# Conformer convolution: first channel half moved between and beside the query/key projections of the second attention kind

## The chip, the cores and the metric

The kernel runs as one launch on one core of a Trainium2 chip. The time is device microseconds of one execution; a smaller one is better. The kernel before took 3023.3 us as the median of three runs (3010.88 to 3023.79).

## The reference, cut to what matters

Two transformer blocks are computed in float32, one after the other. The change lies in the first block, which has two layers (l = 0 and l = 1) over 512 main tokens and 256 context tokens of width 1024; layer 1 needs only the main tokens' result. One layer, cut:

```python
h = rms_norm(x, n1) * (1 + sc1) + sh1          # hc the same for the context
a_b, a_c, a_h, b_v, b_g, c_q, c_k, c_v, d_q, d_k, d_v = split_proj(h @ w_in)
ya = short_conv_mixer(a_b, a_c, a_h, conv_a)
yb = conformer_conv(b_v, b_g, conv_b, conv_b_bias, cln_g, cln_b)
yc = window_attention(apply_rope(q_heads(c_q), ...), ...)
yd = global_attention(apply_rope(rms_norm(q_heads(d_q), qn_g), ...), ...)
x_new = x + g1 * (concat([ya, yb, yc, yd]) @ w_out)
x_new = x_new + g2 * expert_choice_ffn(h2, ...)

def conformer_conv(a, g, w, bias, ln_g, ln_b):
    u = a * sigmoid(g)
    u = dwconv(u, w) + bias                    # depthwise, 31 taps, 256 channels
    return silu(layer_norm(u, ln_g, ln_b))
```

`c_q, c_k, c_v` are the queries, keys and values of the window attention (kind 0 in the kernel), `d_q, d_k, d_v` those of the global attention (kind 1). The 256 channels of the convolution are two halves of 128 (ch = 0 and 1), one partition a channel. The convolution needs nothing of the attention and the attention nothing of it; both end in `y`, which the output projection reads.

## The kernel before

The program is written with a tile framework: engines run their own queues in order, and the order of each queue is fixed when the kernel is built. A scheduler walks all instructions and gives an engine the ready one that stands first in program order, by its own model of durations; so an instruction that comes later in the program can run early, as filler, when all before it wait. Tiles come from pools: an instruction that needs a new tile waits until one of the pool's slots is free.

A matmul of float32 is made of three (`mm3`, L334 to L336): high part by high part, and the two mixed products, from operands split into a rounded high part and a rest. `take_hl` (L253 to L266) takes the next loaded weight tile and splits it: two casts on ACT (L263), two subtractions (L264) on DVE, or the second of them on POOL unless `dve` is set. The raw tile `w`, `wh` and `wl` are slots of one pool, `wp`, of six. Weights come through one list of entries in the order of use (`all_entries`) over SP's queue; `pump` keeps at most `cap` raw tiles issued and not released (2 in this stage).

A layer's first part runs so:

- `qkv_group` (L762): kind 0, then kind 1. Each kind has two weight tiles and six token tiles (four main, two context; I call such a step a position): 24 matmuls into a `pd` tile (a PSUM pool of two), which ACT copies out (L779, L783). For kind 1, DVE then works out the rms norm of the heads (a chain of small instructions, L788 to L793, with L278 to L280 in it) and the rotation (L808, L812), with POOL in between (L798, L816, L817); two positions later PE transposes the result (L826). Between the matmuls stand steps of the modulation vectors (`mods_steps`, L373), each on a 1 MB tile of `ada_w`: 24 in layer 0, 8 in layer 1.
- Attention: `attn_window`, `attn_global` and, in layer 0, `attn_ctx`, 8 units each (24 in layer 0, 16 in layer 1). A unit is scores (L935), maximum (L856), exponential (L862), sums and reciprocal (L866 to L870; L866 and L868 only where there is a sink), scaling of the probabilities (L881 on DVE for one head, L879 on ACT for the other), transposes (L907), copies out of PSUM (L330, L328), and the product with the values (L915).
- Beside it the conformer convolution, a Python generator: `long_conv` (L613). For ch = 0 and 1 and for each set of tokens (512 main, in layer 0 also 256 context): 48 matmuls (`two`, 24 for the values and 24 for the gate, two `pd` tiles), the gate (L625), the product `u` (L627), the middle tap (L630), and 30 further taps. Of those, 16 (14 for the context) are a product on ACT (L642) that POOL adds to `a2` (L644); the other 14 (16) are one instruction of DVE each (L648). POOL adds `a2` in the end (L650). `u`, `a2` and the taps' products share a pool `t2` of 6 slots in layer 0 and 8 in layer 1. From the seventh unit on three steps of the generator are emitted after each unit (START, RATE), and what is left after the last unit.
- `short_conv` (L679): three more weight tiles, each with the same 48 matmuls for each set, and the layer norm of the convolution's result. Then `out_proj`.

So in program order half 0 stands beside the units from the seventh on, and half 1, apart from its first instructions, behind all attention.

Of the kernel before, what the change touches and what calls it, by code (L numbers as in the profile page):

```python
# [1 line left out]

# [46 lines left out]
RATE = (3, 3)  # L49
BTA = 6  # L50
# [68 lines left out]
class Kern:  # L119
# [316 lines left out]
    def all_entries(self):  # L436
        for k in range(8):
            self.ada_entry(0, 0, k)
        for l in range(2):
# [5 lines left out]
            for x in ada[:cut]:  # L445
                self.ada_entry(*x)
            self.dense_entries("w_in", l, 7, 9, (4, 512))
            for x in ada[cut:]:
                self.ada_entry(*x)
            self.dense_entries("w_in", l, 0, 5, (8, 256))  # L450
# [67 lines left out]
    def layer(self, l):  # L518
# [42 lines left out]
        kq = self.qkv_group(l, hT, last, tiles, W)  # L561
        ep = self.phase(ptp=PT[l], p3p=P3[l], qsp=QS)
        sets = [(0, 512)] if last else [(0, 512), (1, 256)]
        conv = self.long_conv(l, hT, y, sets)
# [37 lines left out]
    def two(self, hT, w, m, n):  # L602

        out = []
        for q in range(2):
            pp = self.pd()
# [3 lines left out]
            out.append(pp)  # L610
        return out

    def long_conv(self, l, hT, y, sets):  # L613
# [3 lines left out]
        hb = self.sm(62, "hb", bufs=1)  # L617
        nc.vector.tensor_scalar(hb, self.pvv("cwb", l * 62, 62), 0.5, None, op0=ALU.mult)
        taps = lambda j, n: (slice(max(0, 15 - j), n - max(0, j - 15)), slice(max(0, j - 15), n - max(0, 15 - j)))
        for ch in range(2):  # L620
            w = self.take_hl(dve=WDVE)
            for m, n in sets:
                pv, pg = self.two(hT, w, m, n)
                th = self.t2((n,))
                nc.scalar.activation(out=th, in_=pg[:, :n], func=AF.Tanh, scale=0.5)  # L625
                u = self.t2((n,), s="u")
                nc.vector.scalar_tensor_tensor(u, th, 1.0, pv[:, :n], op0=ALU.add, op1=ALU.mult)  # L627
                ac = y[m](2 + ch)
                col = lambda j: hb[:, ch * 31 + j:ch * 31 + j + 1]
                nc.vector.tensor_scalar(ac, u, col(15), self.pvv("cbb", l * 2 + ch, 1), op0=ALU.mult, op1=ALU.add)  # L630
                yield

                side = SIDE if m == 0 else SIDEC
                for j in range(15 - side, 16 + side):
                    if j != 15:
                        to, fr = taps(j, n)
                        f = self.t2((n,), s="tap")[:, :to.stop - to.start]
                        if j == 15 - side:
                            a2 = self.t2((n,), s="a2")
                            nc.gpsimd.memset(a2[:, 0:16], 0.0)  # L640
                            f = a2[:, to]
                        nc.scalar.activation(out=f, in_=u[:, fr], func=AF.Copy, scale=col(j))  # L642
                        if j > 15 - side:
                            nc.gpsimd.tensor_tensor(a2[:, to], a2[:, to], f, op=ALU.add)  # L644
                            yield
                for j in list(range(15 - side)) + list(range(16 + side, 31)):
                    to, fr = taps(j, n)
                    nc.vector.scalar_tensor_tensor(ac[:, to], u[:, fr], col(j), ac[:, to], op0=ALU.mult, op1=ALU.add)  # L648
                    yield
                nc.gpsimd.tensor_tensor(ac, ac, a2, op=ALU.add)  # L650
# [102 lines left out]
    def qkv_group(self, l, hT, last, tiles, W):  # L753
# [14 lines left out]
        for kind in range(2):  # L768
            if kind == 1:
                W = [self.take_hl() for _ in range(2)]  # L770
            for it, (m, t) in enumerate(order):
# [67 lines left out]
                while done < goal:  # L839
                    next(steps)  # L840
                    done += 1
                MARK("qkv")
# [1278 lines left out]
```

## Time and profile before

| what | value |
|---|---|
| median of the runs | 3023.3 us (3010.88, 3023.3, 3023.79) |
| profiled execution, its own time | 3013.78 us |
| its span, first to last instruction | 3011.8 us |
| mean granted TensorE clock | 0.972 |
| busy share of the span | PE 94%, PEld 60%, DVE 42%, ACT 27%, POOL 15% |
| layer 0: kind 1 of the projections | about 98 to 157 us |
| layer 0: attention and convolution | about 157 to 332 us |
| layer 0: short convolution | about 332 to 385 us |
| layer 1: kind 1 | about 1113 to 1150 us |
| layer 1: attention and convolution | about 1150 to 1318 us |

The profiled execution's own time is 2 us over its span. PE is TensorE's matmuls, PEld its weight loads (which overlap the matmuls), DVE is VectorE, ACT ScalarE, POOL GpSimd, SP the queue of the weight transfers. Times in the rows below are us from the start of the span, durations us unless a row says ns. A clock of 1.00 is TensorE's full clock of 2.4 GHz, 0.50 is 1.2 GHz.

### The profile page before, as it was taken

The page shows a single profiled execution, that of the slowest core. Times are in us where ns is not written, and L with a number is a line of the kernel's source. Part 1 is how long each engine was busy: PE and PEld are TensorE (multiplying, and loading weights), DVE is VectorE, ACT ScalarE, POOL GpSimd, SP SyncE. Part 2 cuts the span into 40 slices and gives each one's busy share as a digit, 9 for nine tenths or more (in the row PEclk, how much of TensorE's full clock was granted, in tenths as well). Part 3 has the DMA queues.
Part 4 walks back from the last instruction along what each step waited for, and adds up shares of the span by engine and source line. Part 5 has one row for each costly group of instructions (what it writes and reads, how often), then busy time and mean ns, then how long its engine had stood idle before and what let it go on. Part 6 is the DMA issues. An engine that isn't in the chain of part 4 may idle for free.

```text
span 3011.8 us, 38597 instructions
## 1 busy us (share of the span) xinstructions
PE 2822.7 (94%) x15736; PEld 1802.0 (60%) x15736; DVE 1279.5 (42%) x2657; ACT 819.9 (27%) x1519; POOL 464.4 (15%) x378
## 2 busy tenths in 40 slices
PE   6989899999999879997999888999999999999998
PEld 3666675444444356674433224788886777888886
DVE  5387754111111157744222225532446483444344
ACT  3266432000000035631000003322236442322222
POOL 2233332111111024331000000222210001100000
PEclk9999899999999989998999999999999999999999
DMA  7710136999999942147999996232231122222222
GB/s 274 273 66 15 43 112 258 411 406 404 394 405 386 362 148 96 43 186 288 426 426 426 426 426 266 86 111 84 91 103 57 68 83 89 93 97 98 84 91 77
DMA packets 103841, 623.13 MB, mean 207 GB/s; under 512 B 11056, under 2 KB 13232, under 8 KB 36592
## 3 DMA queue, kind: packets, MB, share of 16 engines
q1 hardware_dynamic: 89120, 580.82, 48.7%
q0 software_dynamic: 8352, 18.10, 2.3%
q10 hardware_dynamic: 6192, 21.75, 1.9%
q8 instruction: 124, 2.03, 0.3%
q14 instruction: 53, 0.43, 0.0%
HBM read 601.74 MB, written 18.87 MB: 206 GB/s over the span
## 4 chain that ended last, share of the span: by engine, by line
PE 44%; DMA 7%; DVE 3%; ACT 1%; issue 0%; SPq 0%; DVEq 0%; ACTq 0%
PE pd L334 6%; PE pd L335 5%; PE pd L336 5%; PE pb L1242 4%; PE pb L334 3%; PE pa L334 3%; PE pb L335 3%; PE pb L336 3%; PE pa L335 3%; PE pa L336 3%; DMA w<-w_up 3%; PE pd L1279 2%; DMA w<-w_down 2%; DMA w<-w_gate 2%; PE pb L1337 1%; PE pb L1813 1%
## 5 line engine op out<-in xcount | busy, mean ns | idle before, releaser
L1242 PE MATMUL pb<-w,X 128*64 128x512 f32 x2048 | 464.3, 600 | 13.5 <-DMA w<-w_up 7.3
L1242 PEld LDWEIGHTS pb<-w,X 128*64 128x64 f32 x2048 | 150.9, 138 | 310.2 <-issue 268.5
L263 ACT CAST wh<-w 128x1024 fp32r<-128x1024 f32 (+3 forms) x239 | 235.9, 1029 | 360.2 <-issue 125.2
L1279 PE MATMUL pd<-w,hT 128*64 128x512 f32 (+1 forms) x2048 | 303.5, 493 | 6.0 <-DVE hT L330 2.6
L264 DVE TENSOR_TENSOR wl<-w,wh 128x1024 fp32r<-128x1024 f32 (+3 forms) x189 | 229.8, 1236 | 146.7 <-ACT wh L263 140.0
L334 PE MATMUL pd<-hh,wh 128*128 128x512 f32 (+1 forms) x720 | 284.6, 396 | 8.0 <-ACT wh L263 3.9
L336 PE MATMUL pd<-hh,wl 128*128 128x512 f32 (+1 forms) x720 | 283.0, 393 | 0.3 <-DVE wl L264 0.3
L335 PE MATMUL pd<-hl,wh 128*128 128x512 f32 (+1 forms) x720 | 282.9, 393 | 0.0
L1252 ACT ACTIVATE s<-pb 128x512 f32<-128x512 f32 x32 | 19.1, 598 | 694.4 <-PE pb L1242 694.4
L1279 PEld LDWEIGHTS pd<-w,hT 128*64 128x64 f32 (+1 forms) x2048 | 102.4, 123 | 165.7 <-issue 131.7
L264 POOL TENSOR_TENSOR wl<-w,wh 128x1024 fp32r<-128x1024 f32 (+1 forms) x50 | 132.0, 2639 | 412.4 <-ACT wh L263 390.1
L1253 DVE TENSOR_TENSOR s<-s,pb 128x512 f32<-128x512 f32 x32 | 22.0, 687 | 399.5 <-ACT s L1252 399.5
L334 PEld LDWEIGHTS pd<-hh,wh 128*128 128x128 f32 x720 | 138.4, 192 | 38.1 <-ACT wh L263 7.1
L336 PEld LDWEIGHTS pd<-hh,wl 128*128 128x128 f32 x720 | 138.1, 192 | 28.9 <-issue 0.8
L335 PEld LDWEIGHTS pd<-hl,wh 128*128 128x128 f32 x720 | 138.4, 192 | 28.0 <-issue 1.5
L334 PE MATMUL pb<-wh,fh 128*128 128x512 f32 x352 | 138.4, 397 | 0.8 <-DVE x L1674 0.8
L336 PE MATMUL pa<-hh,wl 128*128 128x512 f32 x352 | 139.1, 395 | 0.0
L334 PE MATMUL pa<-hh,wh 128*128 128x512 f32 x352 | 139.1, 395 | 0.0
L335 PE MATMUL pa<-hl,wh 128*128 128x512 f32 x352 | 139.1, 395 | 0.0
L335 PE MATMUL pb<-wl,fh 128*128 128x512 f32 x352 | 138.1, 392 | 0.0
L336 PE MATMUL pb<-wh,fl 128*128 128x512 f32 x352 | 138.1, 392 | 0.0
L1210 POOL DMA_INDIRECT gat<-xd,gi x48 | 47.0, 979 | 573.8 <-PE pa L1224 325.7
(464 smaller groups left out, 4698.1 us busy)
## 6 DMA issues: line engine op xcount, KB each, us to landing
w<-w_up SPq DMA_DIRECT2D x128, 1024.0 KB
w<-w_gate SPq DMA_DIRECT2D x128, 1024.0 KB
w<-w_down SPq DMA_DIRECT2D x128, 1024.0 KB
w<-ada_w SPq DMA_DIRECT2D x48, 1024.0 KB
w<-w_in SPq DMA_DIRECT2D x18, 1024.0 KB
w<-f1g SPq DMA_DIRECT2D x11, 1024.0 KB
w<-f1u SPq DMA_DIRECT2D x11, 1024.0 KB
w<-f2g SPq DMA_DIRECT2D x11, 1024.0 KB
```

What stands on the lines that cost most here:

```text
L263: nc.scalar.copy(hi[:, s], w[:, s])
L264: (nc.gpsimd if i and not (dve or self.dve) else nc.vector).tensor_tensor(lo[:, s], w[:, s], hi[:, s].bitcast(F32), op=ALU.subtract)
L334: nc.tensor.matmul(ps, lhsT=l[0], rhs=r[0], start=first, stop=False)
L335: nc.tensor.matmul(ps, lhsT=l[0], rhs=r[1], start=False, stop=False)
L336: nc.tensor.matmul(ps, lhsT=l[1], rhs=r[0], start=False, stop=last)
L1210: self.nc.gpsimd.indirect_dma_start(out=g, out_offset=None, in_=R["xd"].rearrange("t (h w) -> (t h) w", h=dup), in_offset=bass.IndirectOff ...
L1242: nc.tensor.matmul(pp[h * cap:(h + 1) * cap, 0:w], lhsT=X[:, k], rhs=Wk[:, h * w:(h + 1) * w], start=(k == 0), stop=(k == 7))
L1252: nc.scalar.activation(out=s, in_=pp[:, 0, 0:w], func=AF.Silu)
L1253: nc.vector.tensor_tensor(s, s, pp[:, 1, 0:w], op=ALU.mult)
L1279: nc.tensor.matmul(py[h * cap:(h + 1) * cap, 0:w], lhsT=hT[:, k % nj, k // nj], rhs=Wd[k // 2][:, k % 2, h * w:(h + 1) * w], start=(k == 0 ...
L1337: nc.tensor.matmul(ps[:, t], lhsT=oh[:, (2 * t2 + t) * 128:(2 * t2 + t + 1) * 128], rhs=z[:, i], start=(i == 0), stop=(i == 1))
L1813: nc.tensor.matmul(s_[:, g, :nk], lhsT=qT[0:96, h, n * 128:nk], rhs=kT[0:96, h, 0:nk], start=True, stop=False)
```

## The change

The generator is now made once for each half. `layer` makes `hb` (the taps' weights) itself, makes both generators before the projections, hands the first to `qkv_group`, and chains what is left of it before the second for the attention as before:

```diff
+        hb = self.sm(62, "hb", bufs=1)
+        nc.vector.tensor_scalar(hb, self.pvv("cwb", l * 62, 62), 0.5, None, op0=ALU.mult)
+        conv0, conv = [self.long_conv(l, hT, y, sets, ch, hb) for ch in range(2)]
+        kq = self.qkv_group(l, hT, last, tiles, W, conv0)
+        conv = chain(conv0, conv)
...
         for kind in range(2):
             if kind == 1:
+                next(conv)
                 W = [self.take_hl() for _ in range(2)]
...
+                if kind == 1:
+                    for _ in range(CRATE[l]):
+                        next(conv, None)
```

with `CRATE = (10, 5)`, six positions each: 60 calls in layer 0 for the 58 steps of half 0, 30 in layer 1 for 29. The first call of a generator now makes the matmuls, gate, `u` and middle tap of all sets, and the taps follow:

```diff
+        us = []
+        for m, n in sets:
+            out = None
+            if ch == 0:
+                z = self.pd((2, 256)) if m else self.pb((2, 512))
+                out = [z[:, 0], z[:, 1]]
+            pv, pg = self.two(hT, w, m, n, out)
+            th = self.t2((n,))
+            nc.scalar.activation(out=th, in_=pg[:, :n], func=AF.Tanh, scale=0.5)
+            u = self.t2((n,), s="u")
+            nc.vector.scalar_tensor_tensor(u, th, 1.0, pv[:, :n], op0=ALU.add, op1=ALU.mult)
+            nc.vector.tensor_scalar(y[m](2 + ch), u, col(15), self.pvv("cbb", l * 2 + ch, 1), op0=ALU.mult, op1=ALU.add)
+            us.append(u)
+        yield
+        for (m, n), u in zip(sets, us):
+            ac = y[m](2 + ch)
...
```

For half 0 the main tokens' two results lie in one `pb` tile (the PSUM pool that the attention's scores and the modulation steps use), the context's in one `pd` tile; for half 1 each result has a `pd` tile as before. The weight tile of half 0 moves up in the list of entries, in front of those of kind 1:

```diff
             for x in ada[:cut]:
                 self.ada_entry(*x)
+            self.dense_entries("w_in", l, 0, 1, (8, 256))
             self.dense_entries("w_in", l, 7, 9, (4, 512))
             for x in ada[cut:]:
                 self.ada_entry(*x)
-            self.dense_entries("w_in", l, 0, 5, (8, 256))
+            self.dense_entries("w_in", l, 1, 5, (8, 256))
```

No arithmetic is added or left out.

## Rows read from the trace of the kernel before

**Rows 1.** Busy us of each engine (instructions), clock, DMA share, GB/s, by stretch.
```profile
98.00:157.00 59.00, 55.87 (x287) 32.74 (x287) 28.90 (x113) 13.77 (x34) 17.36 (x22) 0.97 0.80 294
157.00:332.00 175.00, 151.83 (x857) 103.45 (x858) 143.43 (x269) 116.14 (x258) 65.52 (x65) 0.92 0.05 20
...
190.00:230.00 40.00, 34.19 (x200) 23.94 (x200) 39.93 (x65) 29.68 (x63) 24.27 (x19) 0.91 0.01 2
230.00:281.00 51.00, 50.48 (x276) 32.36 (x276) 33.97 (x61) 29.33 (x59) 9.07 (x13) 1.00 0.06 21
281.00:332.00 51.00, 35.11 (x213) 25.07 (x214) 47.75 (x92) 36.06 (x93) 32.05 (x31) 0.80 0.00 1
...
1175.00:1200.00 25.00, 20.70 (x100) 14.28 (x99) 22.71 (x34) 16.72 (x33) 21.73 (x15) 0.80 0.00 1
...
1220.00:1255.00 35.00, 32.38 (x161) 20.56 (x160) 30.89 (x45) 24.71 (x48) 23.09 (x16) 0.95 0.08 31
```

**Rows 2.** The same view in stretches of 10 us around the slow places.
```profile
200.00:210.00 10.00, 8.28 (x48) 7.58 (x49) 9.96 (x16) 6.82 (x14) 6.74 (x6) 0.68 0.00 0
...
290.00:300.00 10.00, 7.31 (x44) 5.61 (x44) 10.00 (x20) 6.48 (x16) 7.61 (x7) 0.83 0.00 0
300.00:310.00 10.00, 2.17 (x14) 1.59 (x16) 9.96 (x14) 5.41 (x17) 7.60 (x6) 0.60 0.00 0
310.00:320.00 10.00, 7.65 (x35) 4.92 (x34) 7.47 (x18) 6.32 (x16) 2.35 (x4) 0.55 0.00 0
...
1180.00:1190.00 10.00, 8.10 (x35) 5.84 (x36) 9.67 (x15) 6.68 (x14) 9.53 (x7) 0.80 0.00 1
1190.00:1200.00 10.00, 7.61 (x36) 5.75 (x34) 9.96 (x12) 5.50 (x10) 7.52 (x5) 0.69 0.01 2
...
1230.00:1240.00 10.00, 10.00 (x45) 5.63 (x43) 7.57 (x13) 6.81 (x13) 4.43 (x5) 0.83 0.00 0
```

**Rows 3.** Groups of 281 to 332 us: busy us, mean ns | idle before, releasers.
```profile
L644 POOL TENSOR_TENSOR a<-a,tap 128x505 f32<-128x505 f32 (+14 forms) x28 | 30.7, 1098 | 42.1 <-ACT tap L642 40.7
...
L648 DVE SCALAR_TENSOR_TENSOR y<-u,hb,y 128x497 f32<-128x497 f32 (+6 forms) x14 | 15.1, 1081 | 0.0
...
L907 PE MATMUL pa<-ct,P 128*128 128x128 f32 x44 | 7.7, 304 | 13.8 <-DVE P L881 12.0 <-DVE ng L858 1.7
```

**Rows 4.** Timeline of DVE around 300 us: start, duration, instruction.
```profile
303.48 1.15 DVE L868 TENSOR_TENSOR sum<-sum,es 128x2 f32<-128x2 f32 x1
...
310.29 0.15 DVE L868 TENSOR_TENSOR sum<-sum,es 128x2 f32<-128x2 f32 x1
```

**Rows 5.** Timeline of POOL in the same stretch.
```profile
303.36 4.23 POOL L644 TENSOR_TENSOR a<-a,tap 128x507 f32<-128x507 f32 x3 [1.00 <-ACT tap L642]
```

**Rows 6.** Timelines of PE and DVE: when half 1's last set is released.
```profile
298.19 0.28 PE L336 MATMUL pd<-hh,wl 128*128 128x256 f32 x1
...
314.63 0.41 DVE L627 SCALAR_TENSOR_TENSOR u<-t,pd 128x256 f32<-128x256 f32 x1
...
313.63 0.78 PE L334 MATMUL pd<-hh,wh 128*128 128x512 f32 x1
```

**Rows 7.** Timeline of PE at the start of kind 1 in layer 0.
```profile
99.59 0.72 PE L334 MATMUL pd<-wh,hh 128*128 128x512 f32 x2 [2.02 <-ACT wh L263]
...
104.21 0.39 PE L334 MATMUL pd<-wh,hh 128*128 128x512 f32 x1
104.44 0.40 PE L335 MATMUL pd<-wl,hh 128*128 128x512 f32 x1
```

**Rows 8.** Timelines of SP and POOL there: the weight tiles of kind 1.
```profile
91.28 0.81 SPq L232 DMA_DIRECT2D w<-w_in  x2
95.67 11.23 SPq L232 DMA_DIRECT2D w<-ada_w  x2
...
100.57 5.98 POOL L264 TENSOR_TENSOR wl<-w,wh 128x1024 fp32r<-128x1024 f32 x2 [18.73 <-ACT wh L263]
```

**Rows 9.** Groups of 98 to 157 us: one line of DVE's chain.
```profile
L278 DVE SCALAR_TENSOR_TENSOR rst<-rsy,hv 128x6 f32<-128x6 f32 x18 | 3.0, 166 | 0.6
```

More of the change, by code (lines that the diff above doesn't have):

```diff
@@ L1 @@
 from contextlib import ExitStack, nullcontext
+from itertools import chain
 import concourse.bass as bass
@@ L49 @@
 RATE = (3, 3)
+CRATE = (10, 5)
 BTA = 6
@@ L560, in layer @@
             y.append(lambda k: ycT[:, k])
-        kq = self.qkv_group(l, hT, last, tiles, W)
+        sets = [(0, 512)] if last else [(0, 512), (1, 256)]
+        hb = self.sm(62, "hb", bufs=1)
[3 more added lines that the diff above has]
+        conv = chain(conv0, conv)
         ep = self.phase(ptp=PT[l], p3p=P3[l], qsp=QS)
-        sets = [(0, 512)] if last else [(0, 512), (1, 256)]
-        conv = self.long_conv(l, hT, y, sets)
         units = [self.attn_window(l, kq, y[0]), self.attn_global(l, kq, y[0])] + ([] if last else [self.attn_ctx(l, kq, y[1])])
@@ L600, in layer, with two @@
             es.close()
-    def two(self, hT, w, m, n):
-        out = []
+    def two(self, hT, w, m, n, out=None):
+        out = out or [self.pd() for _ in range(2)]
         for q in range(2):
-            pp = self.pd()
+            pp = out[q]
             for k in range(8):
@@ L609, in two, with long_conv @@
                          [h(k) for h in hT[m]], k == 0, k == 7)
-            out.append(pp)
         return out
-    def long_conv(self, l, hT, y, sets):
+    def long_conv(self, l, hT, y, sets, ch, hb):
         MARK("conf")
         nc = self.nc
-        hb = self.sm(62, "hb", bufs=1)
-        nc.vector.tensor_scalar(hb, self.pvv("cwb", l * 62, 62), 0.5, None, op0=ALU.mult)
         taps = lambda j, n: (slice(max(0, 15 - j), n - max(0, j - 15)), slice(max(0, j - 15), n - max(0, 15 - j)))
[L620 to L630, printed above, removed]
-                yield
[L633 to L650, printed above, removed]
@@ new lines, in long_conv @@
+        w = self.take_hl(dve=WDVE)
+        col = lambda j: hb[:, ch * 31 + j:ch * 31 + j + 1]
+        us = []
[11 more added lines that the diff above has]
+            us.append(u)
@@ new lines, in long_conv @@
+        yield
+        for (m, n), u in zip(sets, us):
+            ac = y[m](2 + ch)
+            side = SIDE if m == 0 else SIDEC
+            for j in range(15 - side, 16 + side):
+                if j != 15:
+                    to, fr = taps(j, n)
+                    f = self.t2((n,), s="tap")[:, :to.stop - to.start]
+                    if j == 15 - side:
+                        a2 = self.t2((n,), s="a2")
+                        nc.gpsimd.memset(a2[:, 0:16], 0.0)
+                        f = a2[:, to]
+                    nc.scalar.activation(out=f, in_=u[:, fr], func=AF.Copy, scale=col(j))
+                    if j > 15 - side:
+                        nc.gpsimd.tensor_tensor(a2[:, to], a2[:, to], f, op=ALU.add)
+                        yield
+            for j in list(range(15 - side)) + list(range(16 + side, 31)):
+                to, fr = taps(j, n)
+                nc.vector.scalar_tensor_tensor(ac[:, to], u[:, fr], col(j), ac[:, to], op0=ALU.mult, op1=ALU.add)
+                yield
+            nc.gpsimd.tensor_tensor(ac, ac, a2, op=ALU.add)
@@ L751, in early_T, with qkv_group @@
         return F
-    def qkv_group(self, l, hT, last, tiles, W):
+    def qkv_group(self, l, hT, last, tiles, W, conv):
         MARK("qkv_group")
```

## The prediction, before the change was run

> **What bounds the kernel now.** I read the page first (busy shares: PE 94%, no other engine near it), then the busy times by stretch, then the groups and waits of the slow stretches, then the timelines of single engines there. TensorE sets the end nearly everywhere, so what moves matmuls from one place to another moves no time by itself; what counts is where PE idles or runs at 1.2 GHz. From 98 to 157 us (kind 1) it is busy 55.87 of 59 us, with DVE idle half the stretch. From 157 to 332 us (attention beside the convolution) it idles 175 - 151.83 = 23.2 us, at a mean clock of 0.92 [rows 1]. Nearly all of that lies in two places. Between them, from 230 to 281 us, PE is busy 50.48 of 51 us at full clock. In the first place, 190 to 230 us, it idles 5.8 us; in the second, 281 to 332 us, 15.9 us, at a clock of 0.80 [rows 1]. Layer 1 has the same two in small: 4.3 us idle from 1175 to 1200, 2.6 from 1220 to 1255 [rows 1].
>
> What these places have in common is POOL: 24.3 of 40, 32.1 of 51, 21.7 of 25 and 23.1 of 35 us busy, against 9.1 of 51 in the good stretch [rows 1]. That is the addition of taps (28 of 1.1 us in the second place), while DVE's own taps take 1081 ns [rows 3]. The timeline shows why DVE is full: the sum of two numbers per partition (L868) takes 0.15 us when POOL rests and 1.15 us when POOL adds [rows 4]; it ends about a third into the three additions that began at 303.36, where the first of them must end [rows 4, 5]. The softmax chain then comes late, and the transposes of the probabilities wait 12.0 us for DVE's scaling [rows 3]. I call such a stretch a burst. Each half of the convolution makes one burst per set of tokens, the main set's being the long one.
>
> The second burst is worse than the first because PE has no filler in it. The last matmul of half 1's context set runs at 298.19 us, but its two `pd` tiles stay held until DVE makes `u` at 314.63; the next filler, the short convolution's first matmul, starts at 313.63 beside the attention's own [rows 6].
>
> **The change part by part.**
>
> *Matmuls of half 0, moved in front of kind 1.* One `mm3` step takes 104.44 - 104.21 = 0.23 us [rows 7]; 48 of 512 columns are 11.2 us, the context's 48 of half the width an estimated 5.6. So kind 1 ends 17 us later in layer 0 and 11 us in layer 1, and attention has that much less to do. On the path this is nothing, if attention finds other filler. It should: half 1 takes the place of half 0 (17 us), and the three weight tiles of the short convolution (3 x 17 = 51 us, not tied to the taps) follow. Both sets of half 1 now make `u` in the first call, ahead of all their taps, so the held tiles of [rows 6] come free early. Value 0; if that fails, the loss is the second rival.
>
> *Second burst of layer 0, gone from attention.* Idle 15.9 us [rows 1]. The clock's share is busy time by one minus clock, in the three stretches of 10 us: 7.31 x 0.17 + 2.17 x 0.40 + 7.65 x 0.45 = 5.6 us [rows 2]. Together 21.4. Left over: at least the 0.5 us of the good stretch, at most what the first burst costs now, 5.8 + 8.28 x 0.32 = 8.5 us [rows 1, 2]. I take 1.4, nearest to the good stretch because filler is plentiful: gain 20, bounds 13 and 21.
>
> *One of two bursts of layer 1.* The first costs 4.3 + 8.10 x 0.20 + 7.61 x 0.31 = 8.3 us, the second 2.6 + 10.00 x 0.17 = 4.3 [rows 1, 2]. One stays. If it is like the first, the gain is 4.3, otherwise 8.3; I take 4, since it starts where the first did.
>
> *A new wait: the second weight tile of kind 1.* `wp` has six slots. While half 0's matmuls run, `wh` and `wl` of half 0, `wh` and `wl` of kind 1's first tile, the second tile raw and the next `ada_w` tile fill them. The second tile can only be split when half 0's matmuls are over. Before, its split began 1 to 2 us into kind 1 and POOL's two subtractions took 5.98 us together [rows 8], unseen because PE was at 1.2 GHz after its 2.02 us gap [rows 7]. Now PE needs the last quarter after 18 steps = 4.2 us; two casts of about 1 us (the 1 us by which POOL's first subtraction [rows 8] stands behind PE's first step [rows 7]) and a subtraction of 3 us give 5, and behind an addition of taps (1.1 us) 6. So PE waits 0 to 2 us, and a gap of 2 us was followed by cold steps [rows 7]. I take 2.5 in each layer, 5 together (bounds 0 and 8). Behind PE's waiting step stand only kind 1's own matmuls.
>
> *The moved weight transfer.* Half 0's raw tile takes the place of kind 1's first in the pair issued at 91.28 us [rows 8]; the 2.02 us gap [rows 7] now stands in front of half 0 and stays. The pair's other member becomes kind 1's first tile, its second follows when half 0 is split, and the 14 `ada_w` tiles behind start about 10 us later relative to kind 0 but have 17 us more time: DMA is busy 0.80 of the stretch at 294 GB/s [rows 1]. Value 0, bounds 0 and 3.
>
> *Taps of half 0 beside kind 1.* They start as soon as `u` is there, so the burst falls on kind 1's first three or four positions. ACT's and POOL's work fits (kind 1 has them busy 13.8 and 17.4 of 59 us [rows 1]). What can suffer is DVE: a position has 13 instructions with two inputs in SBUF (9 of the kind of L278, 166 ns each [rows 9]). If each is held for 1 us as in [rows 4], a position's chain grows by 13 us. PE needs its result two positions later, which are 12 us off in layer 1 (two of 24 x 0.23 plus a modulation step) and some 16 in layer 0. I take 2 us over both layers, bounds 0 and 17 (the first burst's costs in both layers, 8.5 + 8.3).
>
> The Trainium skill's page "SBUF — State Buffer", section "Who interferes with whom", says that a VectorE instruction with two SBUF inputs contends with a GpSimd instruction that reads SBUF, and that whichever starts second waits for the whole of the other. The trace agrees: L868 at 1.15 against 0.15 us [rows 4]. By that rule alone the burst would not vanish but hold kind 1's chain of small instructions instead, which speaks against the change; the price is the upper bound of 17 just given, and it is the first rival.
>
> *Sum.* 20 + 4 - 5 - 2 = 17 us gained. Against the profiled execution's 3013.8 us (span 3011.8 and 2 around it) that is 2997. This execution lies 9.5 under the median of the runs; all four shown (3010.9, 3013.8, 3023.3, 3023.8) have a mean of 3018, and from there I forecast 3001. What follows (output projection, experts) starts when this part ends and shifts with it.
>
> **The rivals.**
>
> *The burst takes its cost along (no change, chance 0.25).* Kind 1's chain waits as the softmax did, and PE's transposes with it: 24 - 5 - 17 = 2 us gained, 3016. For it: the instructions in kind 1 are of the kind that suffers. Against: there PE depends on them two positions late, and only ACT, which has no such waits in the rows, frees the `pd` tiles.
>
> *Attention starves for filler (slower, chance 0.17).* Half 0's 17 + 11 = 28 us of matmuls now lengthen kind 1 one for one. If the short convolution does not come forward, attention stays as long as its softmax chain makes it, less the burst: 28 - 24 + 7 = 11 us lost, 3029. It decides at one point: whether the short convolution's matmuls start before half 1's taps are through. For it: before, they started at 313.63, 18 us ahead of attention's end, though its weights had long been free to come. Against: what held them was the pair of `pd` tiles [rows 6], which the change frees, and the good stretch shows that filler fills.
>
> *ACT stuck behind taps (slower, chance 0.08).* Products of taps wait for a slot of `t2` until POOL has added; copies out of `pd` queue behind them on ACT. Half 0's 15 additions of the main set take 15 x 1.1 = 17 us in each layer, against positions of 6 to 8 us: at worst one copy per layer is late by 17 - 2 x 6 = 5 us, 10 in all, and with the first rival's cost it is 8 lost, 3026. Against: ACT idles 45 of 59 us in kind 1 [rows 1], and copies stand before taps in program order.
>
> **How the numbers follow.** 0.5 for the forecast, 0.25, 0.17 and 0.08 for the others. The forecast's own bounds are 21 + 8 = 29 gained and, with both new costs at half their bounds, 5 gained: 2989 to 3013. Executions of one kernel spread by 5 us to either side here, and the second rival ends at 3029; so 2984 to 3030. A measurement can tell about 0.5%, 15 us, from no change. The forecast's half gives 0.42 faster and 0.08 within; the first rival 0.04 faster, 0.19 within, 0.02 slower; the other two 0.07 within and 0.18 slower: 0.46, 0.34 and 0.20.
>
> **What would show it.** Right: one burst of POOL in each attention, PE busy to over 95% at full clock in the last 45 us of layer 0's attention; half 0's 96 matmuls between kind 0 and kind 1; a short gap 3 to 5 us into kind 1 that ends with `wl`; the short convolution's first matmul well before attention's end. Wrong: idle time of PE in kind 1 that ends with `qkr` or ACT's copies (first and third rival), attention as long as before less only a few us (second rival), or a second burst that is still there.

## The result, and the profile after

The changed kernel is slower. Its five runs took 3043.18 to 3047.58 us, median 3046.22; five runs of the kernel before beside them took 3010.88 to 3024.38, median 3023.3. The ratio is put at 1.0095, with a 95% interval of 1.0084 to 1.0105 (the two medians alone give 1.0076). I had forecast 3001 and a range to 3030, so both the sign and the range were wrong. Its profiled execution took 3044.1 us (span 3042.1), 30.3 more than that of the kernel before.

The line of engines on its page shows nothing of this: shares are within a point of those before.

```profile
PE 2829.8 (93%) x15736; PEld 1801.5 (59%) x15736; DVE 1292.4 (42%) x2657; ACT 822.7 (27%) x1519; POOL 463.9 (15%) x378
```

So I cut both layers into two stages: **projections** (in layer 0 from the end of kind 0, in layer 1 from the last transposes of the layer's input, early in kind 0, to the last transposes of the rotated results) and **attention** (from there to the first matmul of the expert router's setup, L1083, which stands at the start of the output projection). Columns as in [rows 1]: start and end, length, busy us of PE, PEld, DVE, ACT and POOL, granted clock, DMA share, GB/s. First the kernel before:

```profile
97.40:158.00 60.60, 56.86 (x293) 33.24 (x291) 30.04 (x119) 14.91 (x38) 17.49 (x23) 0.97 0.80 298
158.00:391.90 233.90, 206.37 (x1180) 149.97 (x1177) 179.70 (x341) 132.93 (x286) 77.23 (x69) 0.93 0.08 28
1087.30:1162.20 74.90, 74.00 (x405) 53.60 (x404) 42.81 (x141) 23.26 (x62) 22.78 (x31) 1.00 0.48 169
1162.20:1316.90 154.70, 144.92 (x760) 97.78 (x760) 113.08 (x203) 94.03 (x181) 53.31 (x36) 0.96 0.12 43
```

The changed kernel in the same stages:

```profile
97.40:193.10 95.70, 78.30 (x391) 48.54 (x388) 72.17 (x155) 34.89 (x72) 51.07 (x55) 0.89 0.53 196
193.10:399.20 206.10, 192.99 (x1084) 135.86 (x1082) 140.64 (x306) 114.97 (x252) 42.86 (x37) 0.93 0.08 28
1097.20:1208.10 110.90, 91.95 (x465) 66.28 (x462) 69.58 (x159) 36.32 (x81) 47.15 (x48) 0.92 0.37 133
1208.10:1349.40 141.30, 130.84 (x698) 85.75 (x698) 97.56 (x186) 82.06 (x162) 29.10 (x19) 0.95 0.11 40
```

The projections grew by 35.1 us in layer 0 and 36.0 in layer 1, all of it in kind 1; the matmuls put there are 17 and 11. Attention shrank by 27.8 and 13.4. PE's idle time in the projections (length less busy) went from 3.7 to 17.4 us and from 0.9 to 19.0. Most of it is one wait in each layer. Timeline of PE in the changed kernel (start, duration, instruction, count, and in brackets the idle time before it with what ended it); its lines stand 2 to 13 further down than before (L336 to L338 are the matmuls of `mm3`, L836 the transposes, L826 and L827 the rotated result `qkr`, L280 to L282 the steps that were L278 to L280, L653 POOL's additions, L657 DVE's taps):

```profile
141.68 0.40 PE L338 MATMUL pd<-wh,hl 128*128 128x512 f32 x1
155.66 0.90 PE L836 MATMUL pa<-ct,qkr 128*128 128x128 f32 x3 [13.59 <-POOL qkr L826]
...
1154.37 0.40 PE L338 MATMUL pd<-wh,hl 128*128 128x512 f32 x1
1170.04 0.90 PE L836 MATMUL pa<-ct,qkr 128*128 128x128 f32 x3 [15.27 <-POOL qkr L826]
...
1173.33 0.63 PE L337 MATMUL pd<-wl,hh 128*128 128x512 f32 x1
```

PE has done the matmuls of the third position and stands at the transposes of the first. After the wait a step takes 0.63 us instead of 0.39. DVE and POOL tell why the first position is late. DVE in layer 1:

```profile
1139.80 7.76 DVE L657 SCALAR_TENSOR_TENSOR y<-u,hb,y 128x497 f32<-128x497 f32 x5
...
1147.69 0.54 DVE L798 TENSOR_REDUCE hs<-sq 128x6 f32<-128x384 f32 x1
1148.15 0.90 DVE L657 SCALAR_TENSOR_TENSOR y<-u,hb,y 128x502 f32<-128x502 f32 x1
1148.98 1.25 DVE L800 TENSOR_SCALAR hv<-hs 128x6 f32<-128x6 f32 x1
...
1154.45 1.22 DVE L280 SCALAR_TENSOR_TENSOR rst<-rsy,hv 128x6 f32<-128x6 f32 x1
1155.59 0.73 DVE L657 SCALAR_TENSOR_TENSOR y<-u,hb,y 128x501 f32<-128x501 f32 x1
1156.24 1.21 DVE L281 TENSOR_TENSOR rst<-rst,rsy 128x6 f32<-128x6 f32 x1
...
1164.68 0.15 DVE L280 SCALAR_TENSOR_TENSOR rst<-rsy,hv 128x6 f32<-128x6 f32 x1
...
1166.28 0.56 DVE L803 TENSOR_TENSOR qk<-src,rsy 128x384 f32<-128x384 f32 x1
```

and POOL:

```profile
1139.44 24.65 POOL L653 TENSOR_TENSOR a<-a,tap 128x505 f32<-128x505 f32 x15
1164.89 1.27 POOL L659 TENSOR_TENSOR y<-y,a 128x512 f32<-128x512 f32 x1 [0.80 <-POOL a L653]
...
1169.27 0.72 POOL L826 TENSOR_TENSOR qkr<-r,r 128x256 f32<-128x256 f32 x1 [1.21 <-DVE r L822]
1169.94 0.46 POOL L827 TENSOR_TENSOR qkr<-r,r 128x128 f32<-128x128 f32 x1
```

For 24.65 us POOL adds almost without a pause. In that time six numbers per partition cost DVE 1.2 us, and between nearly any two of these small instructions stands a tap. When the additions end, at 1164.09, the next of them takes 0.15 us. From the start of L798 to that of L803 the chain takes 18.6 us.

### The profile page after: what moved, and what is told of

Its sections match the earlier page's. It is cut to its first block, busy times and chain, and to the rows that moved or that the text cites. A ratio compares the mean times of both kernels' runs of the same rounds, so it can differ in the third digit from the quotient of the medians.

```text
span 3042.1 us, 38566 instructions
## 1 busy us (share of the span) xinstructions
PE 2829.8 (93%) x15736; PEld 1801.5 (59%) x15736; DVE 1292.4 (42%) x2657; ACT 822.7 (27%) x1519; POOL 463.9 (15%) x378
## 4 chain that ended last, share of the span: by engine, by line
PE 42%; DMA 8%; DVE 3%; ACT 1%; issue 0%; SPq 0%; DVEq 0%; ACTq 0%; POOLq 0%
PE pd L336 5%; PE pd L337 5%; PE pd L338 5%; PE pb L1255 4%; PE pb L336 3%; PE pa L336 3%; PE pb L338 3%; DMA w<-w_down 3%; PE pa L337 3%; PE pb L337 3%; PE pa L338 3%; DMA w<-w_up 3%; PE pd L1292 2%; DMA w<-w_gate 2%; PE pb L1826 1%; PE pb L1350 1%
## 5 line engine op out<-in xcount | busy, mean ns | idle before, releaser
L1255 PE MATMUL pb<-w,X 128*64 128x512 f32 x2048 | 463.2, 597 | 15.1 <-DMA w<-w_up 9.2
L336 PE MATMUL pd<-hh,wh 128*128 128x512 f32 (+1 forms) x688 | 269.4, 392 | 10.0 <-ACT wh L265 3.9
L337 PE MATMUL pd<-hl,wh 128*128 128x512 f32 (+1 forms) x688 | 268.9, 391 | 0.0
L338 PE MATMUL pd<-hh,wl 128*128 128x512 f32 (+1 forms) x688 | 268.7, 391 | 0.3 <-DVE wl L266 0.3
L336 PEld LDWEIGHTS pd<-hh,wh 128*128 128x128 f32 x688 | 130.6, 190 | 40.3 <-ACT wh L265 7.1
L338 PEld LDWEIGHTS pd<-hh,wl 128*128 128x128 f32 x688 | 130.8, 190 | 26.4 <-DVE wl L266 0.7
L337 PEld LDWEIGHTS pd<-hl,wh 128*128 128x128 f32 x688 | 130.8, 190 | 26.3 <-issue 1.5
L336 PE MATMUL pb<-wh,fh 128*128 128x512 f32 x352 | 138.7, 398 | 0.8 <-DVE x L1687 0.8
L338 PE MATMUL pa<-hh,wl 128*128 128x512 f32 x352 | 139.1, 395 | 0.0
L336 PE MATMUL pa<-hh,wh 128*128 128x512 f32 x352 | 139.1, 395 | 0.0
L338 PE MATMUL pb<-wh,fl 128*128 128x512 f32 x352 | 138.0, 392 | 0.0
```

Of the source, the lines that this page charges most:

```text
L336: nc.tensor.matmul(ps, lhsT=l[0], rhs=r[0], start=first, stop=False)
L337: nc.tensor.matmul(ps, lhsT=l[0], rhs=r[1], start=False, stop=False)
L338: nc.tensor.matmul(ps, lhsT=l[1], rhs=r[0], start=False, stop=last)
L1255: nc.tensor.matmul(pp[h * cap:(h + 1) * cap, 0:w], lhsT=X[:, k], rhs=Wk[:, h * w:(h + 1) * w], start=(k == 0), stop=(k == 7))
```

## The experiments

L0 and L1 in the table are the lengths of the two layers in the profiled execution, both stages together, in us. Each ratio is to the kernel before on the same chip, with its 95% interval; the changed kernel was not run again there. The kernel before had medians of 3014.3 to 3016.8 us on the five chips of the experiments. A profiled execution can lie 10 us off the median of its kernel (e1 and e5 under it, e3 over it), and so can L0 and L1; differences of a few us in them alone show nothing. e1, e7, e8 and e16 leave out additions or taps and so part of the arithmetic.

| run | median us | ratio (interval) | L0 | L1 |
|---|---|---|---|---|
| before | 3015 | 1 | 294.5 | 229.6 |
| after | 3046 | 1.0095 (1.0084, 1.0105) | 301.8 | 252.2 |
| e1_no_add0 | 3014.1 | 0.9996 (0.9984, 1.0008) | 278.6 | 238.2 |
| e2_dve0 | 3022.6 | 1.0022 (1.0013, 1.0032) | 286.8 | 246.6 |
| e3_lag4 | 3043.8 | 1.0085 (1.0063, 1.0108) | 306.3 | 252.7 |
| e4_hold | 3073.5 | 1.0173 (1.0140, 1.0205) | 326.6 | 258.7 |
| e5_gen | 3024.2 | 1.0035 (1.0020, 1.0050) | 292.0 | 232.8 |
| e6_l0only | 3027.7 | 1.0043 (1.0027, 1.0060) | 300.5 | 241.8 |
| e7_before_noadd | 2974.1 | 0.9856 (0.9840, 0.9873) | 269.2 | 215.5 |
| e8_after_noadd | 2995.9 | 0.9930 (0.9913, 0.9947) | 270.6 | 235.4 |
| e9_lag4_tq18 | 3034.2 | 1.0063 (1.0045, 1.0080) | 293.2 | 254.2 |
| e10_l0_dve0 | 3009.7 | 0.9979 (0.9970, 0.9989) | 290.0 | 233.0 |
| e11_before_dve | 2997.0 | 0.9935 (0.9919, 0.9952) | 284.9 | 220.6 |
| e12_before_side4 | 2992.1 | 0.9915 (0.9895, 0.9935) | 274.6 | 228.8 |
| e13_after_side4 | 3036.8 | 1.0064 (1.0046, 1.0081) | 295.1 | 260.7 |
| e14_l1only | 3041.4 | 1.0090 (1.0071, 1.0108) | 294.9 | 255.4 |
| e15_before_side40 | 2987.6 | 0.9905 (0.9889, 0.9922) | 274.8 | 220.6 |
| e16_after_notaps0 | 2976.5 | 0.9866 (0.9848, 0.9883) | 266.8 | 218.3 |
| e17_hold2 | 3038.2 | 1.0077 (1.0056, 1.0097) | 303.8 | 247.1 |
| e18_hold2_side40 | 3033.7 | 1.0064 (1.0047, 1.0081) | 293.7 | 244.7 |

**e1_no_add0.** Edit: half 0's additions only.

```diff
-                        nc.gpsimd.tensor_tensor(a2[:, to], a2[:, to], f, op=ALU.add)
+                        if ch:
+                            nc.gpsimd.tensor_tensor(a2[:, to], a2[:, to], f, op=ALU.add)
```

> Half 0's additions on POOL (15 of the main set, 13 of the context) are left out; the products of ACT are still made, the order of DVE's queue in kind 1 stays the same. Theory LOCK (a POOL addition holds each of DVE's small instructions, and each then costs as much as an addition): the chain of kind 1's first position falls from 19 us (layer 1) and 14 us (layer 0) to 10 or less, PE's idle times of 15.3 and 13.6 us fall under 3 each, and the time falls to 3005 to 3020. Rival QUEUE (what delays the chain is the DVE tap that stands between any two of its instructions): the chain keeps 13 taps of up to 0.7 us and 5 us of its own, 14 us; idle of 8 to 12 us stays in each layer, 3035 to 3045.

DVE's order is the same, yet the same chain takes 9.2 us instead of 18.6, and a step 0.16 us instead of 1.22. The taps are held too: the five in front of the chain take 3.83 us instead of 7.76. DVE of e1:

```profile
1113.96 3.83 DVE L658 SCALAR_TENSOR_TENSOR y<-u,hb,y 128x497 f32<-128x497 f32 x5
...
1117.91 0.54 DVE L799 TENSOR_REDUCE hs<-sq 128x6 f32<-128x384 f32 x1
...
1121.35 0.16 DVE L280 SCALAR_TENSOR_TENSOR rst<-rsy,hv 128x6 f32<-128x6 f32 x1
1121.47 0.74 DVE L658 SCALAR_TENSOR_TENSOR y<-u,hb,y 128x501 f32<-128x501 f32 x1
...
1127.09 0.56 DVE L804 TENSOR_TENSOR qk<-src,rsy 128x384 f32<-128x384 f32 x1
```

Its stages:

```profile
97.40:177.00 79.60, 75.98 (x395) 48.60 (x392) 52.81 (x155) 33.31 (x72) 19.93 (x27) 0.98 0.65 239
177.00:376.00 199.00, 187.13 (x1084) 133.02 (x1082) 141.19 (x306) 114.81 (x252) 43.30 (x37) 0.97 0.09 29
1071.30:1168.20 96.90, 91.26 (x466) 66.26 (x465) 56.34 (x159) 36.03 (x81) 23.70 (x33) 0.98 0.43 151
1168.20:1309.50 141.30, 130.81 (x697) 85.82 (x697) 97.59 (x186) 81.96 (x162) 29.14 (x19) 0.95 0.11 40
```

The long waits are gone (1.94 us is left of the 15.27); idle time in the projections is 3.6 and 5.6 us. LOCK is shown: half 0's additions cost the changed kernel 1% (1.0095 to 0.9996), some 30 us. But the projections of layer 1 are not as before (5.6 us idle against 0.9), and the whole kernel, rid of one burst, is no faster than before: something else costs as much as that burst did.

**e2_dve0.** Edit, with no final addition where `side` is 0:

```diff
-            side = SIDE if m == 0 else SIDEC
+            side = (SIDE if m == 0 else SIDEC) if ch else 0
```

> All 30 taps of half 0 are single instructions of DVE; nothing of half 0 runs on ACT's taps or on POOL. LOCK: no instruction of the chain is held; taps of 0.4 to 0.7 us stand between the small ones, so a chain takes 9 to 12 us in more positions than before, under the 12 to 16 us that PE allows; idle under 5 us in each layer, 3010 to 3030. QUEUE: twice as many taps stand in DVE's queue, the idle times stay or grow, 3046 or more.

The time is within LOCK's range, the idle time is not: 9.0 us in the projections of layer 0 and 15.4 in layer 1, where under 5 were expected. Of the 15.4, waits of 1.6 and 5.0 us end with `qkr`; two others end with a modulation weight's transfer (3.1) and with ACT's copy (2.4). Taps alone hold the chains of more positions; LOCK named too small a price for DVE's queue, and that queue is not all of it.

**e3_lag4, e9_lag4_tq18.** Edit (18 in place of 14 in e9):

```diff
-TQ = (10, 10)
+TQ = (14, 14)
...
-                if len(late) > 2:
+                if len(late) > (4 if kind else 2):
```

> Kind 1's transposes stand four positions later in PE's queue instead of two (the pool of their tiles has 14 slots instead of 10); additions and taps as in the changed kernel. If PE's idle time comes from the place of the transposes in its in-order queue, behind a chain that is 10 to 15 us late once (both theories), 12 us more of slack takes it to under 4 us in each layer, and the time falls to 3015 to 3030. Rival LOAD: DVE is late in all positions, because the work is too much for it; then the idle time comes back behind a later position and the time stays at 3040 or more.

> As the kernel with transposes four positions later, but with 18 slots in the pool of their tiles instead of 14. There the idle time of layer 0 came back as a wait for the copy into that pool (8.1 us), because slots stay held until the late chain has read them. If what matters is how many positions PE may run ahead (slack), half a position more of slots takes 3 to 6 us of idle time away in each layer: 3030 to 3037. Rival LOAD (DVE is late in every position): the idle time stays within 2 us in sum, 3040 or more.

With 14 slots nothing that the intervals can tell is gained, as LOAD said; but the wait is at another place, as it did not say. PE of e3:

```profile
171.40 0.80 PE L336 MATMUL pd<-wh,hh 128*128 128x512 f32 x1 [8.11 <-ACT src L793]
```

ACT of e3 shows what the copy out of `pd` stands behind:

```profile
160.42 0.50 ACT L651 ACTIVATE a<-u,hb 128x249 f32<-128x249 f32 x1 [13.44 <-POOL a L649]
...
170.48 0.50 ACT L651 ACTIVATE tap<-u,hb 128x250 f32<-128x250 f32 x1 [1.85 <-POOL a L653]
170.89 0.46 ACT L793 COPY src<-pd 128x384 f32<-128x384 f32 x1
```

Products of the context set's taps stand in front of it in ACT's queue. ACT idled 13.44 us for POOL to clear `a2` (L649), behind the late chain's own instructions in POOL's queue, and then up to 1.85 us for an addition before most of the further products. That is the mechanism of the prediction's third rival, which the longer wait for `qkr` covers in the changed kernel. My reason in the expectation of e9 (slots of the pool) is refuted there: with 18 slots the same wait is 8.12 us. e9's ratio of 1.0063 is in the range that slack was to bring, but its interval overlaps e3's, and the projections' idle time does not fall (18.7 and 16.4 us against 17.2 and 15.1 in e3). So the lower time does not come from there, and what it comes from is not shown.

**e4_hold.** Edit: half 0's taps read a copy of `hb` that depends on kind 1's last keys.

```diff
+        nc.vector.scalar_tensor_tensor(hb2, kh[:, kt * 128:kt * 128 + 62].bitcast(F32), 0.0, hb, op0=ALU.mult, op1=ALU.add)
+        hbs.append(hb2)
...
-CRATE = (10, 5)
+CRATE = (0, 0)
```

> Half 0's matmuls, gate and u stand in front of kind 1 as in the changed kernel, but its 30 taps depend on a result of kind 1's last position, so that none runs in kind 1. LOCK and QUEUE: no idle time of over 2 us in kind 1; attention has half 0's and half 1's bursts, with the short convolution as filler: 3010 to 3030, I say 3018. Rival MOVE: the cost comes from the matmuls' new place (filler taken from attention, weight tiles, the pb tile): 3035 or more with no idle time in kind 1.

Kind 1 is clean, as LOCK said, and the time is the worst of all, as MOVE said. PE idles at the start of attention, with no filler:

```profile
188.37 2.18 PE L954 MATMUL pb<-kh,qs 64*128 64x512 f32 x6 [10.37 <-ACT P L881]
...
197.81 1.51 PE L926 MATMUL pa<-ct,P 128*128 128x128 f32 x6 [6.93 <-DVE P L900]
```

ACT of e4 shows where the filler is: half 1's weight tile is split at 226 us, behind the products of half 0's taps. The kernel before split half 0's tile at 159 (the figure in e17's expectation) and half 1's at 163.

```profile
225.60 0.49 ACT L657 ACTIVATE tap<-u,hb 128x249 f32<-128x249 f32 x1
225.99 1.98 ACT L265 CAST wh<-w 128x1024 fp32r<-128x1024 f32 x2
```

and ACT of the kernel before:

```profile
162.99 1.99 ACT L263 CAST wh<-w 128x1024 fp32r<-128x1024 f32 x2
```

**e17_hold2, e18_hold2_side40.** Edit: as e4, with half 1's weight tile split before those taps; e18 has the taps shared out as in e15.

```diff
+        next(conv)
...
         w = self.take_hl(dve=WDVE)
+        if ch:
+            yield
```

> As the kernel with half 0's taps held until kind 1 is done (3073), but half 1's weight tile is split at the start of attention, before those taps. In the first one ACT's cast of that tile stood behind the products of the held taps, at 226 us instead of 159, and PE had no filler from 177 to 230 us. ACT QUEUE (that cast is what made it slow): most of the loss goes, 3015 to 3035. Rival MOVE: the matmuls are missing in attention whichever they are; 3055 or more.

> The last one with 7 additions on POOL per set in layer 0 and none in layer 1, which without the move took 2988. If the move of the matmuls alone is free, as where half 0's taps were left out, 2985 to 2995, no better than without it; if filler is lost, 3005 or more.

The early split takes more than half of e4's loss away, but e17 ends 3 us past what ACT QUEUE allowed, and e18 is 1.6% over e15, which it was to equal: on the side of lost filler. Held taps all begin with attention, beside a softmax that has lost their matmuls as filler (in e17 PE waits 6.1 and 3.9 us there at 188 and 211 us). These two runs do not separate the matmuls' place from the taps' new start.

**e5_gen, e6_l0only, e14_l1only.** Edits: e5 has the new generator with nothing moved; e6 and e14 have the move (with its weights, tiles and CRATE) under `if l == 0` and `if l == 1`:

```diff
             if kind == 1:
-                next(conv)
+                if l == 0:
+                    next(conv)
```

> Only the new generator: u of both sets in its first call, ahead of the taps; nothing of half 0 is moved, the list of weights and the pd tiles are those of the kernel before. Theory HELD (in layer 0 the pair of pd tiles held until u leaves attention without filler): the second stretch of idle time gets shorter by 5 us or more, 3003 to 3010 where the kernel before has 3015. Rival: filler is not what the second stretch lacks, the softmax chain is late anyway; within 4 us of the kernel before. Layer 1 has one set and should not move at all.

> The change is made in layer 0 alone; layer 1 has the order of the kernel before. From the two traces, layer 0 of the changed kernel loses 8 us and layer 1 loses 23: if the layers are independent, the time is 8 us over the kernel before, 3019 to 3027, and layer 1 is as long as before to 2 us. Rival: part of layer 1's loss comes from layer 0 (late weights, a late start); then it stays in part, 3030 or more.

> The change in layer 1 alone; layer 0 has the new generator, but nothing moved. LOCK beside FILLER (layer 1 has no transfer or stretch that gains from the move, its attention loses as much as before with one burst less): 3033 to 3040, 16 to 20 over the generator alone. Rival: the layers' losses come from their sequence (the earlier stage shifts the later one); then 3028 or less.

HELD fails on the time: from 281 to 332 us PE idles 11.2 us instead of 15.9, but layer 0 of the profile (of the fastest of its ten runs) is only 2.5 us shorter, and the kernel is 0.35% slower, some 10 us, over runs that spread from 3014 to 3038. The scheduler puts some instructions of layer 1 (on DVE, ACT and PE) in another order than before, which I had not expected; whether that is the whole 0.35% was not tested. The move comes on top of it: 0.08% for layer 0 (e6 against e5) and 0.55% for layer 1 (e14 against e5), 2 and 17 us, and the sum 0.35 + 0.08 + 0.55 = 0.98% is the loss of the changed kernel (0.95%). The intervals are 0.15 to 0.2% wide to either side, so layer 0's share can't be told from none; layer 1's can. The layers add up within that, and layer 1 is the one that loses. e6 ends 0.7 us and e14 1.4 us over the range given, and that layer 1 of e6 would be as long as before to 2 us did not hold (last section).

**e7_before_noadd, e8_after_noadd.** Edit, in both halves (here of the changed kernel):

```diff
                     if j > 15 - side:
-                        nc.gpsimd.tensor_tensor(a2[:, to], a2[:, to], f, op=ALU.add)
                         yield
```

> The kernel before with all of POOL's additions of taps left out, in both halves and both layers (the products stay). Theory BURST (idle time and cold clock in attention come from POOL's additions): of the 32.6 us that layer 0 loses between kind 1 and the output projection and the 14.2 of layer 1 at most 10 and 5 stay; 30 us less than the kernel before, 2980 to 2990. Rival CHAIN (in attention PE waits for the softmax chain whatever POOL does): less than 12 us are gained.

> The changed kernel with all of POOL's additions of taps left out, as in the last one. BURST: what attention still loses without half 0's additions (18.1 us in layer 0, 16.1 in layer 1) comes from half 1's; it falls to 10 and 5, and the time to 2995. Rival FILLER (layer 1's attention loses because it has 11 us less of other matmuls): layer 1 keeps 10 us or more of it, and the kernel is slower than the kernel before with the additions left out by 10 us or more.

BURST is shown for the kernel before, with a larger price than expected: 40.7 us, of them 25 in layer 0 and 14 in layer 1. The changed kernel loses 50 to its additions. Without any, it is still 22 us behind, 20 of them in layer 1 (235.4 against 215.5), which is what FILLER said, though the time of 2996 is the one that BURST named; the next run asks whether for FILLER's reason.

**e16_after_notaps0.** Edit, beside that of e8:

```diff
-        for (m, n), u in zip(sets, us):
+        for (m, n), u in zip(sets, us) if ch else ():
```

> The changed kernel with all 30 other taps of half 0 left out (products, additions and DVE's), and half 1's additions left out; half 0's matmuls, gate and u stand between the kinds. The kernel before without any addition took 2974, the changed one 2996. QUEUE (DVE's taps between the chain's small instructions hold kind 1): the idle time of layer 1's kind 1 falls from 5.6 to about 1, and 6 us are gained. FILLER (the matmuls are missing at the end of layer 1's attention, where PE waits for the norm of the convolution): 8 us or more of it stay; 2984 to 2991. Rival: without taps in kind 1 the move is free, 2974 or less.

Layer 1 of e8:

```profile
1060.80:1157.70 96.90, 91.27 (x466) 65.92 (x464) 56.33 (x159) 35.96 (x81) 23.67 (x33) 0.98 0.43 151
1157.70:1296.20 138.50, 129.62 (x709) 87.18 (x710) 94.50 (x190) 86.06 (x170) 12.44 (x8) 0.97 0.12 44
```

and of e16:

```profile
1060.20:1145.90 85.70, 84.52 (x447) 61.99 (x446) 44.74 (x145) 25.51 (x65) 22.35 (x31) 1.00 0.45 160
1145.90:1278.50 132.60, 129.73 (x717) 87.48 (x717) 89.72 (x186) 81.73 (x162) 6.42 (x4) 0.99 0.12 42
```

Without half 0's taps the projections are 10.8 us longer than before (74.9), which are the matmuls, with 1.2 us idle, and all but 2 us of the 22 are gone. QUEUE named the cause but a third of its price; FILLER expected 8 us to stay and is refuted in this form. The last rival (without taps the move is free) missed its bound by 2.5 us, and e16's interval overlaps that of e7. e16 also leaves out work that the kernel before does in attention; in e7, which has those taps there, PE idles 2.9 us in layer 1's attention, as in e16. Beside kind 1 the same taps cost 19 us even with POOL silent: by the profiles 11 in layer 1's projections, 6 in its attention, where PE waits 3.95 us for the convolution's norm, and 4 in layer 0.

**e10_l0_dve0, e13_after_side4.** Edits: e10 joins those of e6 and e2 (the latter for layer 0). e13 and e12 have 7 additions per set:

```diff
-SIDE = 8
+SIDE = 4
...
-SIDEC = 7
+SIDEC = 4
```

> The change in layer 0 alone, with all 30 taps of half 0 there on DVE; layer 1 has the order of the kernel before. LOCK: layer 0 gains about 7 us, as it did where both layers were so, and layer 1 is that of the new generator alone (0 to 10 us more): 3008 to 3018. Rival QUEUE: the taps on DVE hold the chain as the additions did; 3025 or more.

> The changed kernel with 7 additions on POOL for each set of each half instead of 15 (13 for the context); the other taps on DVE. LOCK: the chain of kind 1's first position is held by half as many additions; idle time and cold clock of that stretch (22 us in each layer) fall by a third to a half in each, and the time to 3015 to 3025, but stays 20 us or more over the kernel before with the same split of taps (2992). Rival: the move pays once additions are few; then it is at 2992 or less.

With half the additions the long waits halve (6.9 and 7.2 us), but second ones of 4.2 and 4.7 us appear (more taps are on DVE; that this is why was not tested): idle time in the projections falls by 3 and 4 us only, and the time ends above what was expected. e10 is the one full version with the move that beats the kernel before, by 0.2%.

**e11_before_dve, e12_before_side4, e15_before_side40.** Edits in the kernel before: e11 has both constants at 0 and no final addition, e12 both at 4; e15:

```diff
-                side = SIDE if m == 0 else SIDEC
+                side = 0 if l else 4
```

> The kernel before with all 30 taps on DVE in both halves and both layers: no product on ACT, no addition on POOL. LOCK: 41 us are to be had without the additions; DVE gets some 16 taps of 0.73 us for each main set and 14 of 0.45 for each context set, 36 us in layer 0 and 23 in layer 1, which makes it about 88% busy in attention, so that part of the gain is lost again: 2980 to 3005. QUEUE: DVE becomes the bound, and its small instructions stand behind taps: 3015 or more.

> The kernel before with 8 products on ACT and 7 additions on POOL for each set instead of 16 and 15 (14 and 13 for the context); the other taps are on DVE. LOCK: half of the additions, so about half of the 41 us that they cost, less what the taps cost on DVE: 2992 to 3008. QUEUE: 3015 or more.

> The kernel before with 7 additions per set in layer 0 and none in layer 1 (there all taps on DVE): the better one of the two splits that were run for each layer. Layer 0 gained 18 us with 7 additions, layer 1 7 us with none: 2988 to 2993 if the layers add up; over 2997 if not.

All fell into LOCK's ranges (e15 half a microsecond below its own). e15 moves nothing, only gives POOL fewer additions, and is the fastest full version here: 0.9905, 27 us under the kernel before.

## Why the prediction was wrong, step by step

*Taps of half 0 beside kind 1 (2 us, bounds 0 and 17): the step that failed.* The mechanism was named, as the first rival. Two things in the term were wrong: what I set the chain's growth against, and what the growth is made of. I took the whole distance of two positions, 12 us, as slack. But the chain without any tap uses most of that distance. In the kernel before, DVE, POOL and PE in layer 1, for the first position:

```profile
1122.88 0.56 DVE L788 TENSOR_REDUCE hs<-sq 128x6 f32<-128x384 f32 x1 [4.82 <-ACT sq L786]
...
1125.90 0.56 DVE L793 TENSOR_TENSOR qk<-src,rsy 128x384 f32<-128x384 f32 x1
```

```profile
1129.59 0.46 POOL L817 TENSOR_TENSOR qkr<-r,r 128x128 f32<-128x128 f32 x1
```

```profile
1133.50 0.49 PE L826 MATMUL pa<-ct,qkr 128*128 128x128 f32 x3
```

The result is ready at 1130.05 and PE takes it at 1133.50: 3.5 us of slack, not 12. The trace that I had holds these rows, and I did not read them.

In the changed kernel the path from the squares (ready at 1142.25) to the end of `qkr` (1170.40) takes 28.2 us, 21.0 more than the 7.2 before. Of these, 5.4 pass before the chain begins, behind taps in DVE's queue, and 15.6 in the chain (18.6 - 3.0). e1 parts them by cause: without the additions 1.5 and 6.2 are left, 7.7 us of taps in the queue, which my sum did not have at all; the additions make the other 3.9 and 9.4. These 13.3 us agree with the 13 of my sum, in part by luck: I had counted only the chain's instructions with two inputs, and the trace has the taps and three instructions with one input held as well. PE stood at the transposes 12.5 us after the squares and could begin when the first part of `qkr` was there, 27.8 us after them; 27.8 - 12.5 = 15.3, the wait in the timeline, and the sign of being wrong that the prediction named. The projections' excess over the matmuls is 35.1 - 17 = 18 us in layer 0 and 36.0 - 11 = 25 in layer 1 (part of this is attention's work that fills in), against my upper bound of 17 for both. The waits are 13.6 and 15.3 of it; the rest, shorter waits, steps at the low clock and that work, I did not take apart.

The rule of the Trainium skill, "SBUF — State Buffer", section "Who interferes with whom", was the one to follow. By it each small instruction with two SBUF inputs waits for a whole addition: 1.22 us against 0.16 without additions agrees, and so does L798, a reduction, which the page says never contends on this chip (0.54 in both). L800, with one SBUF input, took 1.25 against 0.17; the page has such instructions contend in a two-port mode only, which the profile doesn't show. L276 and L277 did likewise (1.26 and 1.25 against 0.16 and 0.17).

*Second burst of layer 0 (gain 20).* Half of it came: attention shrank by 27.8, of which 17 are the moved matmuls, so 11. Its last 45 us are as forecast (316.6 to 361.6: PE busy 43.0 us at full clock). The burst that stays costs more than the 1.4 us I left for it, and more than the 8.5 of my bound. The view by stretch of the changed kernel:

```profile
250.00:290.00 40.00, 34.66 (x124) 22.50 (x124) 26.94 (x42) 21.61 (x44) 22.37 (x23) 0.68 0.00 0
275.00:290.00 15.00, 15.00 (x46) 9.69 (x47) 5.42 (x9) 7.70 (x16) 4.89 (x8) 0.50 0.00 0
1220.00:1250.00 30.00, 23.84 (x115) 16.50 (x115) 26.20 (x40) 17.87 (x35) 20.23 (x15) 0.77 0.10 36
```

In 250 to 290 us PE idles 5.3 us and loses 34.66 x 0.32 = 11 to the clock, 16 together. After the idle time the clock was at 1.2 GHz, and it stayed there although PE was busy again: for all of 275 to 290 us in the second row. I had read the price of a burst from the first place in [rows 1] as if every burst cost that; the last section shows by how much the clock alone can change it. I had also counted on plentiful filler. It was there, but behind: PE waited 3.7 us, until 254.89, for DVE's part of a query before it could make the scores, and the short convolution's next step, at 256.25, stood after them in PE's queue.

*One of two bursts of layer 1 (gain 4).* 13.4 - 11 = 2.4 us; idle time of that stage is 10.5, before 9.8. The remaining burst (1220 to 1250, 6.2 us idle) costs what two did, with 11 us less of other matmuls beside it.

*Second weight tile (-5).* Mis-sized: PE waits 0.1 us for it in layer 0 and 0.4 in layer 1. *Moved transfer (0)*: right, no new wait for it (the gap at 99.59 us is 1.85, before 2.02). *Moved matmuls (0)*: e16 agrees for matmuls without taps; e17 and e18 don't settle it for full arithmetic.

The sum in the prediction's own terms: 18 + 25 - 11 - 2.4 = 29.6 us lost, against 30.3 in the profile. It is made of the stages' lengths, so it shows where the time went and not why; the why rests on e1, e8 and e16.

*The rivals.* The first had the right mechanism and the right sign of the evidence, and ended at "no change" because it took over my bound of 17 and the full gain of 24 in attention. The second did not happen: the short convolution's first matmul in layer 0 came at 240.8 us, 121 before attention's last product ends at 361.6, and that was its deciding point. The third is refuted for the changed kernel, where PE waits for `qkr` and not for ACT's copies; it shows in e3 and e9, where the transposes stand later.

## What to carry to other kernels

Before work is moved beside a chain that another engine waits for, read from the trace when the chain's result is ready and when it is taken; only that difference is slack, not the distance in the schedule. An engine that idles half of a stretch is not free if what runs there is a row of dependent small instructions: each filler instruction between them, and each GpSimd addition across them, is paid once per link. Where a resource conflict is the cost, doing less of the conflicting work (half the additions, e12 and e15) gained more than any move of it.

## What was not expected of the hardware

e5 and e6 have the same order of instructions in layer 1's attention, on DVE, ACT and POOL and also on PE. Their two profiled executions differ by 9 us in that stage. e5:

```profile
1159.70:1317.90 158.20, 144.32 (x765) 97.65 (x765) 119.72 (x204) 93.90 (x181) 51.49 (x36) 0.98 0.12 42
```

and e6:

```profile
1167.70:1335.10 167.40, 154.01 (x765) 103.73 (x765) 120.66 (x204) 93.96 (x181) 52.43 (x36) 0.91 0.11 39
```

Idle time is alike (13.9 and 13.4 us); the clock is not. e5's execution is the fastest of its ten, and its other runs reach 3037.9 us, so this may be a difference of executions and not of kernels. Why the clock stayed low in one and not in the other was not tested.

The low clock also lasted differently after waits in the changed kernel: after 15.27 us without work (1170.04) PE's steps were back at 0.40 us by 1175.7, while after a wait of 1.64 us (269.52) they still took 0.63 us or more at 283.6, and the clock was 0.50 up to 290 us (the row for 275 to 290 us).
